# The first weight pieces of a sub-layer: an own slab for the first, a new order of low parts and normalisations, half pieces, and unread products

## The chip, the cores and the metric

The kernel runs on one core of a Trainium2 chip. The metric is the device time of one execution in microseconds. PE is TensorE, DVE is VectorE, ACT is ScalarE, POOL is GpSimd, and SP is the SyncE queue that issues the transfers of weights.

## The reference, cut to what matters

One decoder layer over 256 tokens of 2048 channels, batch 1, all in fp32: three sub-layers, each modulated by products of the condition `c` with `w_cond`.

```python
mod = (silu(c) @ w_cond + b_cond).reshape(B, 3, 3, 2048)     # shift, scale, gate of each sub-layer
u = x * (1 + mod[:, 0, 1]) + mod[:, 0, 0]
h = (silu(u @ w1) * (u @ w3)) @ w2                            # FFN1, inner width 5632
x = layer_norm(ALPHA * x + 0.5 * (1 + mod[:, 0, 2]) * h)
u = x * (1 + mod[:, 1, 1]) + mod[:, 1, 0]
q, k, v, s = split(u @ w_in)                                  # mixer
h = concat([diff_attention(q, k, v), s5(s)]) @ w_out
x = layer_norm(ALPHA * x + (1 + mod[:, 1, 2]) * h)
...                                                           # FFN2 as FFN1, then the output
```

## The kernel before, in words

**Products.** An fp32 operand is held as two rounded parts, `hi` and `lo` for weights, `Uh` and `Ul` for activations (`Hh`/`Hl`, `Ah`/`Al` further on). A product is three on PE: hi with Uh, hi with Ul, lo with Uh.

**The stream.** Weights come in pieces of 128 x 1024 (512 KB), one `Job` each, in one fixed order over all three sub-layers. SP loads a piece into a ring of four `raw` buffers (`load_to`). `split_to(k)` lets ACT write `hi` (a cast) for all pieces up to number k and puts the subtraction that makes `lo` on a list; `pay` lets DVE work that list off, and after each issues the load of one more raw buffer. The rings of hi and lo have four buffers each. After each job, `split_to(done + 4)` runs and `drain` adds DVE work that has time: `gv`, a multiply-and-sum of `c` with a 128 x 1024 piece of `w_cond`. How much is added follows `GVM`, a share of PE's time. The order of each engine's instructions is exactly the order in which this program issues them; an engine that waits holds everything behind it.

**A boundary between sub-layers.** The last block of columns (`last_block`) is done for token half 0 over all pieces, then for token half 1 in two parts, so that half 0's residual (`r`, `Y`), statistics and normalisation run beside half 1's products. Half 0 is normalised on ACT, half 1 on DVE, 512 columns at a time (four `TENSOR_SCALAR` on `Y`); `NOW` says how many of the four are done at once. Then `turn` transposes Y (products with `ident`): for a pair of 128-column blocks (k), first of token half 0, then of token half 1. `put` makes the operands from the transposed block: ACT writes `uf`, ACT or DVE casts it to `Uh`, DVE subtracts to `Ul`. The first two turns cover k 0 to 3, and "turn 2" and "turn 3" below cover k 4 and 5, and 6 and 7. After the first two turns come the first jobs of the next sub-layer, with later turns between them.

**First jobs.** The mixer begins with 16 jobs for `s` (`mk_s`); one job multiplies 128 columns of weights with k 0 to 7 (24 products 256 wide), so job 0 of the mixer needs turns 2 and 3, which are called in the midst of it by `between`. An FFN job multiplies two k with 512 columns (12 products 512 wide): jobs 0 and 1 need k 0 and 1, jobs 2 and 3 need k 2 and 3.

**Other names.** `slab` is a pool of twelve 128 x 2048 buffers; `pslab` is one of a phase. `Z_AT` is a table of the jobs after which Y gets its residual input (the `SCALAR_TENSOR_TENSOR Y<-X,Y`); `QUIET` is the number of last jobs of a sub-layer that run without the limit on DVE work. At the start, 32 narrow products of `early` with `scT` make the first shift, before any U is there.

Of the kernel before, what the change touches and what calls it, by code (L numbers as in the profile page):

```python
# [37 lines left out]
GV_RING = 52  # L38
NT2 = 20
LIM = (3.0, 100.0, 100.0, 100.0)  # L40
GVM = (0.57, 0.65, 0.85, 0.4)
LAG = 8.0
S5_WAIT = 1.7
BG_AT = 70
# [8 lines left out]
S5_AT = 17  # L53
S5_STEP = 4
X_AT = (239, 240, 244, 250)
Z_AT = (242, 246, 251, 256)
NOW = (4, 4)
QUIET = 3
RW = (8, 3, 64)
MAGIC = 12582912.0  # L60
NEG = -1.0e30
# [56 lines left out]
def tile_layer(tc, A, out):  # L118
    nc = tc.nc
    V, S, PE, SP, GP = Meter(nc.vector), nc.scalar, Meter(nc.tensor), nc.sync, nc.gpsimd  # L120
    with ExitStack() as ctx:
# [8 lines left out]
        def psum():  # L130
            return psp.tile([128, 512], F32, tag="ps", name="ps")
# [38 lines left out]
        for k, v in shapes.items():  # L170
# [9 lines left out]
        scT = small([128, NK], "scT", 1)  # L180
        onesr = small([1, 128], "onesr", 5, F32R, tag="w1")
        V.tensor_copy(onesr, ones)
        ch, cl = ([ring.tile([128, CH], F32R, tag=n, name="c" + n, bufs=AHEAD)[0:1, :] for _ in range(2)]
                  for n in ("hi", "lo"))
        for h in range(2):
# [18 lines left out]
        st = {"raw": RAW, "split": 2, "lim": None, "gv_max": 0.0, "gv_credit": 0.0, "s5_at": 0.0}  # L204

        gv_order = [(u, kt) for u in UNITS for kt in range(NS)]
        gv_tiles, gv_n = {}, {"load": 0, "done": 0, "cap": NS}
# [21 lines left out]
        def gv_step():  # L231
            n = gv_n["done"]
            gv_load(n + (8 if n < GV_RING else GVB))
            t = gv_tiles.pop(n)
            u, j = gv_order[n]
            if j == 0:
                st["acc"] = small([128, NS], "acc")
                if n < GV_RING:
                    V.memset(st["acc"], 0.0)
            w = t.shape[-1]  # L240
            gv_n["done"] += w // 1024
            if n == 0:
                st["shift"] = p = psum()[:, 0:1]
                for k in range(NK):
                    PE.matmul(p, t[:, k * 128:(k + 1) * 128], scT[:, k:k + 1], start=k == 0, stop=k == NK - 1)
            else:
                c0 = 0 if w > 1024 else j % 2 * 1024
                V.scalar_tensor_tensor(out=t, in0=t, scalar=1.0, in1=sc[:, c0:c0 + w], op0=ALU.mult, op1=ALU.mult,
                                       accum_out=st["acc"][:, j:j + 1])
                pay_late()  # L250
            n, j = gv_n["done"] - 1, j + w // 1024 - 1
            if n < 4 * NS and j % 8 == 7:
                finish(u, st["acc"], j // 4 - 1, j // 4 + 1)
            elif n >= 4 * NS and j == NS - 1:
                gv_end(u, st.pop("acc"))
# [138 lines left out]
        def pslab(name, dt=F32):  # L394
            return st["ph"].tile([128, D], dt, tag="pslab", name=name)
# [264 lines left out]
        class Stream:  # L660
            def __init__(self):
                self.jobs, self.q, self.raws, self.parts = [], [], {}, {}
                self.ld = self.sp = self.done = 0
                self.limit = 10 ** 6
                self.due, self.owed = {}, []

            def later(self, n, f):
                self.due.setdefault(self.done + n, []).append(f)
# [12 lines left out]
            def split_to(self, k, whole=True):  # L681
                while self.sp < min(k, len(self.q), self.limit):
                    self.load_to(self.sp + 1)
                    raw = self.raws.pop(self.sp)
                    if len(self.q) - 6 <= self.sp < len(self.q) - 4:
                        x = pslab("hilo", F32R)
                        hi, lo = x[:, 0:CH], x[:, CH:2 * CH]
                    else:
                        hi = ring.tile([128, CH], F32R, tag="hi", name="hi", bufs=AHEAD)
                        lo = ring.tile([128, CH], F32R, tag="lo", name="lo", bufs=AHEAD)  # L690
                    S.copy(hi, raw)  # L691
                    self.owed.append((lo, raw, hi))
                    self.parts[self.sp] = (hi, lo)
                    self.sp += 1
                    if whole:
                        self.pay()
# [41 lines left out]
        def kx(tiles, k, t0=0, t1=T):  # L738
            return tiles[k // 8][:, (k % 8) * T + t0:(k % 8) * T + t1]
# [12 lines left out]
        def between(k):  # L752

            if k in mid:
                mid.pop(k)()
# [30 lines left out]
        def last_block(B, ops, db, sub):  # L786

            held = []

            def mk(k0, first, last, src, hold=True):  # L790
                def mm(hi, lo):
                    if first:
                        B["pd"], B["whole"] = [psum(), (psum(), psum())], True
                    form_b1(B["pd"][0], hi, lo, *ops(), k0, 0, first, last)
                    held.append((hi, lo, k0))
                    if not last:
                        return
                    whole = "whole" in B
                    residual(0, db, B["pd"][0])
                    ln_token(sub, 0)  # L800
                    for j, p in enumerate(B["pd"][1]):
                        for i, (h, l, k) in enumerate(held):
                            form_b1(p, h, l, *ops(), k, 1, i == 0 and whole, i == len(held) - 1, 256 * j, 256 * j + 256)
                        if j == 1:
                            stream.split_to(stream.done + 2, False)
                        residual(1, db, p, 256 * j, 256 * j + 256)
                    held.clear()
                    ln_token(sub, 1)
                return Job(mm, src, hold=hold)
            return mk  # L810

        def halves(w, h):
            return w[:, h * CH:(h + 1) * CH]
# [65 lines left out]
            for x, n in zip(st["gb"], ("lng", "lnb")):  # L879
                SP.dma_start(x[:, cs], A[n][sub:sub + 1, cs].to_broadcast([128, 1024]))  # L880

        def turn(ks, then):

            ps = {}
            for k2 in ks:
                for t in range(2):
                    st.pop(("norm", k2 // 2, t), lambda: None)()
            for t in range(2):
                for k2 in ks:
                    if t == 0:  # L890
                        ps[k2] = psum()
                    for i in range(2):
                        PE.transpose(ps[k2][:, i * 256 + t * 128:i * 256 + (t + 1) * 128],
                                     st["Y"][t][:, (2 * k2 + i) * 128:(2 * k2 + i + 1) * 128], ident)
                    if t == 1:
                        then(k2, ps[k2])

        def turn_mod(blk):
            def then(k2, p):
# [217 lines left out]
        def mixer():  # L1117
# [12 lines left out]
            def mk_s(t, hf):  # L1130
                def mm(hi, lo):
                    if hf == 0 and t % 2 == 0:
                        M["ps", t // 2] = psum()
                    M["pt"] = p = M["ps", t // 2][:, (t % 2) * T:(t % 2 + 1) * T]
                    for k in range(8):
                        between(8 * hf + k)
                        w = hi[:, k * 128:(k + 1) * 128]
                        PE.matmul(p, w, kx(st["U"][0], 8 * hf + k), start=hf == 0 and k == 0 and t % 2 == 0,
                                  stop=False, skip_group_check=True)
                        PE.matmul(p, w, kx(st["U"][1], 8 * hf + k), start=False, stop=False, skip_group_check=True)  # L1140
                    for k in range(8):
                        PE.matmul(p, lo[:, k * 128:(k + 1) * 128], kx(st["U"][0], 8 * hf + k), start=False,
                                  stop=hf == 1 and k == 7, skip_group_check=True)

                def post():
                    s = w1([128, 4, 64], "sT")
# [4 lines left out]
                    if t % 4 == 3:  # L1151
# [3 lines left out]
                        for i in range(4):  # L1155
# [1 line left out]
                                M["U4"][32 * i:32 * i + 32, h * 1024:(h + 1) * 1024]  # L1157
                                .rearrange("p (g c) -> p g c", c=64),
                                sD[h * 512:(h + 1) * 512, i, :].rearrange("(g p) c -> p g c", p=32))
                return Job(mm, halves(A["win_a"][t], hf), post if hf else None)  # L1160

            def mk_qk(h, which, hf):
                def mm(hi, lo):
# [327 lines left out]
                 ffn(A["f2w13"], A["f2w2"], 6, [(0, 8), (8, 16)], NT2, KEEP[1])]  # L1491
        for p in parts:
            stream.add(p)
        st["U"] = pairs("U")
        xT = [slab("xT"), slab("xT")]

# [62 lines left out]
        stream.run(4 * NT1 - BG_AT)  # L1559
        bg5.extend(rest)  # L1560
        new_stats()
        stream.run(len(parts[0]) - 4 * NT1 - QUIET)
        drain_s5()
        st["lim"] = None
        stream.run(QUIET)
        stream.flush()
        open_phase("ph1")


        st["X"] = st["Y"]  # L1570
        st["U"] = pairs("U")
        turn(range(2), turn_mod(3))
        mid[2] = lambda: turn((2,), turn_mod(3))
        mid[4] = lambda: turn((3,), turn_mod(3))
        for i in range(4):
            stream.later(1 + i, lambda i=i: turn((4 + i,), turn_mod(3)))
        affines(0, slab, AFF[0])
        new_stats()
        st["lim"], st["gv_max"] = LIM[1], GVM[1]
        stream.run(len(parts[1]) - QUIET)  # L1580
        st["lim"] = None
        stream.run(QUIET)
        stream.flush()
        open_phase("ph2")

# [5 lines left out]
        def kept(k2, p):  # L1591
            q = k2 // 2
            S.copy(xT[:, (k2 % 4) * 512:(k2 % 4 + 1) * 512], p)
            if k2 % 2:
                st["xT", 6, q] = xT[:, (q % 2) * 1024:(q % 2 + 1) * 1024]
                if ("ready", 6, q) in st:
                    modulate(6, q)
        turn(range(2), turn_mod(6))
        stream.later(0, lambda: turn((2,), turn_mod(6)))
        stream.later(1, lambda: turn((3,), turn_mod(6)))  # L1600
        for i in range(4):
            stream.later(2 + i, lambda i=i: turn((4 + i,), kept))
        affines(1, pslab, AFF[1])
        new_stats()
        st["lim"], st["gv_max"] = LIM[2], GVM[2]
# [73 lines left out]
```

## Time and profile before

| | us |
|---|---|
| runs: median (lowest to highest of 3) | 1914.42 (1912.57 to 1918.12) |
| the profiled execution | 1912.22 |
| its span, first to last instruction | 1910.4 |
| PE busy | 1858.5 |
| DVE busy | 1488.1 |
| ACT busy | 889.4 |

Times in the profile are us from the start of the span. A row of the timeline gives start, duration, engine, line, operation, tiles (out<-in), shapes and the number of instructions in a row; in brackets stand the idle time of the engine ahead of it and what ended it. The recorded duration of a product overlaps the next one, so the time that a product takes is read from start to start. The two boundaries lie at about 783 (FFN1 to mixer) and 1148 us (mixer to FFN2).

### The profile page before, as it was taken

Reading aid. Unit: us, or ns where it says so; the run is one execution under the profiler, and the core shown is the slowest. Engines: PE = TensorE matmul, PEld = TensorE weight load, DVE = VectorE, ACT = ScalarE, POOL = GpSimd, SP = SyncE. Lnnn points to the kernel's source line nnn. Section 1 sums busy time; section 2 is a strip of 40 time slices with the busy share of each in tenths; the row PEclk is TensorE's granted clock in tenths of the full one; section 3 lists DMA queues with packets and bytes.
Section 4 is the critical chain, followed back from the end, with each engine's and each line's share of the span. In section 5 each row is a group of like instructions: output and inputs, shape, how many; then the busy total and the mean of one; then the engine's idle time right before and its main releaser. Section 6 shows DMA issues by size and latency. Waiting matters only on the chain.

```text
span 1910.4 us, 25429 instructions
## 1 busy us (share of the span) xinstructions
PE 1858.5 (97%) x9326; PEld 1567.5 (82%) x9326; DVE 1488.1 (78%) x2255; ACT 889.4 (47%) x1211; POOL 65.0 (3%) x119
## 2 busy tenths in 40 slices
PE   6999999999999999899999998999999999999996
PEld 5888878888888888889999886888888888888885
DVE  6889899978888979888998987887876555445468
ACT  3544444465445433634457635544444444344442
POOL 0000000000000000111210000000000000000000
PEclk9999999999999999999999998999999999999998
DMA  9999878889899888798988885998887555565563
GB/s 375 363 338 315 296 247 292 295 306 309 305 347 326 308 323 312 280 337 294 313 268 311 283 309 202 339 357 275 294 279 249 187 188 191 194 215 187 191 233 110
DMA packets 151935, 532.36 MB, mean 279 GB/s; under 512 B 21841, under 2 KB 23297, under 8 KB 150657
## 3 DMA queue, kind: packets, MB, share of 16 engines
q1 hardware_dynamic: 137234, 495.32, 74.3%
q0 software_dynamic: 6512, 23.89, 3.7%
q10 hardware_dynamic: 8064, 11.54, 1.7%
q8 instruction: 73, 1.20, 0.2%
q14 instruction: 52, 0.43, 0.1%
HBM read 513.34 MB, written 17.33 MB: 278 GB/s over the span
## 4 chain that ended last, share of the span: by engine, by line
PE 87%; DVE 6%; DMA 4%; ACT 2%; issue 1%; POOL 0%; SPq 0%; DVEq 0%; ACTq 0%; POOLq 0%
PE ps L106 87%; DVE lo L106 2%; DVE Y L106 2%; DMA raw<-in_f1w_dram 1%; DVE gv L106 1%; ACT hi L691 1%; DMA early<-in_w_cond_dram 1%; DMA raw<-in_wout_dram 0%; DMA U<-sD 0%; DVE st L106 0%; DVE r L106 0%; DMA sD<-sT 0%; DMA early<-in_wc_dram 0%; ACT Y L865 0%; DVE early L106 0%
## 5 line engine op out<-in xcount | busy, mean ns | idle before, releaser
L106 DVE TENSOR_TENSOR lo<-raw,hi 128x1024 fp32r<-128x1024 f32 x630 | 766.3, 1222 | 342.1 <-ACT hi L691 338.5
L691 ACT CAST hi<-raw 128x1024 fp32r<-128x1024 f32 x630 | 661.4, 1053 | 705.8 <-PE ps L106 461.0
L106 PE MATMUL ps<-hi,Uh 128*128 128x512 f32 x1472 | 583.7, 397 | 16.7 <-ACT Uh L318 9.7
L106 PE MATMUL ps<-hi,Ul 128*128 128x512 f32 x1472 | 577.5, 392 | 0.8 <-DVE Ul L106 0.8
L106 PE MATMUL ps<-lo,Uh 128*128 128x512 f32 x1472 | 457.4, 392 | 1.3 <-DVE lo L106 1.3
L106 PEld LDWEIGHTS ps<-hi,Uh 128*128 128x128 f32 x1472 | 278.7, 189 | 77.8 <-ACT Uh L318 10.4
L106 PEld LDWEIGHTS ps<-lo,Uh 128*128 128x128 f32 x1472 | 278.4, 189 | 60.9 <-DVE lo L106 2.0
L106 PEld LDWEIGHTS ps<-hi,Ul 128*128 128x128 f32 x1472 | 279.0, 190 | 58.1 <-DVE Ul L106 1.9
L106 DVE SCALAR_TENSOR_TENSOR gv<-gv,sc 128x1024 f32<-128x1024 f32 x258 | 314.2, 1219 | 1.4 <-DMA gv<-in_w_cond_dram 1.3
L106 PE MATMUL ps<-hi,Hh 128*128 128x512 f32 (+1 forms) x716 | 274.6, 385 | 0.0
L106 PE MATMUL ps<-hi,Hl 128*128 128x512 f32 (+1 forms) x716 | 273.6, 383 | 0.0
L106 PE MATMUL ps<-lo,Hh 128*128 128x512 f32 (+1 forms) x716 | 216.5, 384 | 1.8 <-DVE lo L106 1.8
L106 PEld LDWEIGHTS ps<-lo,Hh 128*128 128x128 f32 x716 | 133.0, 188 | 29.1 <-DVE lo L106 2.6
L106 PEld LDWEIGHTS ps<-hi,Hh 128*128 128x128 f32 x716 | 134.5, 188 | 26.8 <-issue 0.4
L106 PEld LDWEIGHTS ps<-hi,Hl 128*128 128x128 f32 x716 | 134.6, 188 | 26.0
L106 PE MATMUL ps<-Uh,hi 128*128 128x256 f32 x384 | 97.9, 292 | 2.4 <-ACT sT L1147 1.8
L106 PE MATMUL ps<-Ul,hi 128*128 128x256 f32 x384 | 95.7, 286 | 0.1
L106 PEld LDWEIGHTS ps<-Uh,hi 128*128 128x128 f32 x384 | 74.2, 193 | 6.2 <-ACT sT L1147 2.7
L106 PEld LDWEIGHTS ps<-Ul,hi 128*128 128x128 f32 x384 | 74.2, 193 | 0.8 <-DVE Ul L106 0.7
L1010 ACT CAST Hh<-ps 128x512 fp32r<-128x512 f32 x44 | 25.8, 587 | 78.6 <-PE ps L106 78.6
L106 PE MATMUL ps<-Uh,lo 128*128 128x256 f32 x384 | 53.9, 283 | 0.0
L106 DVE TENSOR_TENSOR Hl<-ps,Hh 128x512 fp32r<-128x512 f32 x44 | 30.3, 688 | 30.0 <-ACT Hh L1010 29.7
(229 smaller groups left out, 1393.4 us busy)
## 6 DMA issues: line engine op xcount, KB each, us to landing
raw<-in_f1w_dram SPq DMA_DIRECT2D x264, 512.0 KB, 6.0
raw<-in_f2w_dram SPq DMA_DIRECT2D x264, 512.0 KB, 4.7
gv<-in_w_cond_dram SPq DMA_DIRECT2D x258, 512.0 KB, 7.1
raw<-in_win_a_dram SPq DMA_DIRECT2D x48, 512.0 KB, 6.0
raw<-in_wout_dram SPq DMA_DIRECT2D x32, 512.0 KB, 5.8
early<-in_w_cond_dram SPq DMA_DIRECT2D x28, 512.0 KB, 7.6
s5m<-scrB POOLq DMA_DIRECT2D x8, 1024.0 KB, 8.4
raw<-in_win_v_dram SPq DMA_DIRECT2D x16, 512.0 KB, 4.8
```

The lines of the kernel that those rows point to most:

```text
L106: return f(*a, **k)
L691: S.copy(hi, raw)
L1010: S.copy(hh, p)
```

## The change

Five things change. (1) `warm(n)` issues n products 128 x 512 of a small constant tile `wr` into a PSUM buffer that nothing reads: 16 in the opening, and at each boundary 11 or 12 between the transposes of token half 0 and those of half 1, and 3 behind the latter. (2) The first piece of the mixer and of FFN2 (`firsts`) gets hi and lo in a slab of its own, `hilo`, ahead of the last residual of half 0, and one piece more is cast by ACT at the second part of half 1. (3) `first_turn` replaces the first two turns: of half 1 only the first 512 columns are normalised before them; then follow the lo of job 1's piece, the second normalisation, the casts and lo's of the next pieces, and the last two normalisations. (4) In the mixer the first four jobs do k 0 to 3, with turns 2 and 3 behind the second and third, and then k 4 to 7 of all four; turns 4 to 7 come two jobs later, and in FFN2 every later turn one job later. (5) `Z_AT`, `QUIET` and `GVM` get other numbers.

```diff
-GVM = (0.57, 0.65, 0.85, 0.4)
+GVM = (0.57, 0.68, 0.85, 0.4)
-Z_AT = (242, 246, 251, 256)
-NOW = (4, 4)
-QUIET = 3
+Z_AT = (242, 246, 250, 254)
+NOW = (4, 1)
+QUIET = (6, 5)
+S_LATER = 3
+WARM = dict(opening=16, mixer=(11, 3), ffn=(12, 3))
...
+        def warm(n):
+            p = psum()
+            for _ in range(n):
+                PE.engine.matmul(p, wr[:, 0:1].to_broadcast([128, 128]), wr.unsqueeze(1).to_broadcast([128, 16, 32]),
+                                 start=True, stop=True)
...
                 for k in range(NK):
                     PE.matmul(p, t[:, k * 128:(k + 1) * 128], scT[:, k:k + 1], start=k == 0, stop=k == NK - 1)
+                warm(WARM["opening"])
...
-                    if len(self.q) - 6 <= self.sp < len(self.q) - 4:
-                        x = pslab("hilo", F32R)
+                    if len(self.q) - 6 <= self.sp < len(self.q) - 4 or self.sp in self.firsts:
+                        x = (slab if self.sp in self.firsts else pslab)("hilo", F32R)
...
                     whole = "whole" in B
+                    stream.split_to(stream.done + 2)
                     residual(0, db, B["pd"][0])
...
                         if j == 1:
-                            stream.split_to(stream.done + 2, False)
+                            stream.split_to(stream.done + 3, False)
...
+        def first_turn(blk, idle):
+            turn(range(2), turn_mod(blk), idle)
+            stream.pay()
+            st.pop(("norm", 1, 1))()
+            stream.split_to(stream.done + AHEAD)
+            for q in (2, 3):
+                st.pop(("norm", q, 1))()
...
+                    if hf or t >= AHEAD:
+                        some(p, hi, lo, range(8), hf == 0 and t % 2 == 0)
+                        return
+                    some(p, hi, lo, range(4), t % 2 == 0)
+                    M.setdefault("held", []).append((p, hi, lo))
+                    between(t)
+                    if t == AHEAD - 1:
+                        for i, x in enumerate(M.pop("held")):
+                            some(*x, range(4, 8), False)
+                            stream.split_to(stream.done + 2 + i)
...
-        turn(range(2), turn_mod(3))
-        mid[2] = lambda: turn((2,), turn_mod(3))
-        mid[4] = lambda: turn((3,), turn_mod(3))
+        first_turn(3, WARM["mixer"])
+        mid[1] = lambda: turn((2,), turn_mod(3))
+        mid[2] = lambda: turn((3,), turn_mod(3))
         for i in range(4):
-            stream.later(1 + i, lambda i=i: turn((4 + i,), turn_mod(3)))
+            stream.later(S_LATER + i, lambda i=i: turn((4 + i,), turn_mod(3)))
...
-        turn(range(2), turn_mod(6))
-        stream.later(0, lambda: turn((2,), turn_mod(6)))
-        stream.later(1, lambda: turn((3,), turn_mod(6)))
+        first_turn(6, WARM["ffn"])
+        stream.later(1, lambda: turn((2,), turn_mod(6)))
+        stream.later(2, lambda: turn((3,), turn_mod(6)))
```

On PE at boundary 2, before, the transposes follow one another and job 0 has a hi and lo of the ring:

```order
L106 MATMUL ps_10805<-ident_76,Y_2700 128x128 [waits Activation_49]
L106 MATMUL ps_10805<-ident_76,Y_2700 128x128
L106 MATMUL ps_10808<-ident_76,Y_2700 128x128 x2
L106 MATMUL ps_10805<-ident_76,Y_2701 128x128 [waits DVE_49]
L106 MATMUL ps_10805<-ident_76,Y_2701 128x128
L106 MATMUL ps_10808<-ident_76,Y_2701 128x128 x2
L106 MATMUL ps_10836<-hi_10772,Uh_10800 128x512 [waits DVE_49]
```

At the same place of the changed kernel (Y_2719 is token half 0, Y_2720 half 1):

```order
L108 MATMUL ps_10841<-ident_76,Y_2719 128x128 [waits Activation_49]
L108 MATMUL ps_10841<-ident_76,Y_2719 128x128
L108 MATMUL ps_10844<-ident_76,Y_2719 128x128 x2
L216 MATMUL ps_10847<-wr_98 128x512 x12
L108 MATMUL ps_10841<-ident_76,Y_2720 128x128 [waits DVE_49]
L108 MATMUL ps_10841<-ident_76,Y_2720 128x128
L108 MATMUL ps_10844<-ident_76,Y_2720 128x128 x2
L216 MATMUL ps_10880<-wr_98 128x512 x3
L108 MATMUL ps_10904<-hilo_10730,Uh_10836 128x512 [waits DVE_49]
```

The unread products stand where PE had nothing to do, and job 0 reads its weights from the slab.

On ACT behind boundary 2, before, from the second put on (uf_10855 is turn 2's; the three hi that follow are of jobs 1 to 3):

```order
L743 ACTIVATE uf_10827<-ps_10808,bt6_135,gs6_132 128x256
L745 CAST Uh_10800<-uf_10827 128x256 [waits Activation_49]
L743 ACTIVATE uf_10855<-ps_10850,bt6_135,gs6_132 128x256 [waits PE_49]
L743 ACTIVATE uf_10859<-ps_10850,bt6_135,gs6_132 128x256 [waits DVE_49]
L745 CAST Uh_10800<-uf_10859 128x256 [waits Activation_49]
L691 CAST hi_10863<-raw_10607 128x1024 [waits DMAHW7_49]
L691 CAST hi_10869<-raw_10631 128x1024 [waits DMAHW0_49]
L691 CAST hi_10875<-raw_10666 128x1024 [waits DMAHW2_49]
```

And in the changed kernel (hi_10888 to hi_10918 are of jobs 2 to 4, uf_10946 is turn 2's):

```order
L755 ACTIVATE uf_10876<-ps_10844,bt6_137,gs6_134 128x256
L757 CAST Uh_10836<-uf_10876 128x256 [waits Activation_49]
L703 CAST hi_10888<-raw_10676 128x1024 [waits DMAHW1_49]
L703 CAST hi_10894<-raw_10704 128x1024 [waits DMAHW3_49]
L703 CAST hi_10918<-raw_10733 128x1024 [waits DMAHW4_49]
L755 ACTIVATE uf_10946<-ps_10941,bt6_137,gs6_134 128x256 [waits PE_49]
```

The casts stand ahead of turn 2's uf instead of behind it.

On DVE at the end of FFN1, before, between the last but one and the last residual of token half 0 (r_6654):

```order
L106 SCALAR_TENSOR_TENSOR Y_2700<-X_6148,Y_2700 128x512 [waits DMAHW0_49]
L106 SCALAR_TENSOR_TENSOR Y_2701<-X_6149,Y_2701 128x512 [waits DMAHW1_49]
L106 TENSOR_TENSOR lo_6574<-raw_6485,hi_6573 128x1024 [waits DMAHW5_49,Activation_49]
L106 TENSOR_TENSOR lo_6601<-raw_6503,hi_6600 128x1024 [waits DMAHW6_49,PE_49,Activation_49]
L106 TENSOR_TENSOR lo_6625<-raw_6524,hi_6624 128x1024 [waits DMAHW0_49,PE_49,Activation_49]
L106 TENSOR_TENSOR r_6654<-ps_6579,G_6147 128x512 [waits PE_49]
```

In the changed kernel:

```order
L108 TENSOR_TENSOR lo_6593<-raw_6504,hi_6592 128x1024 [waits DMAHW5_49,Activation_49]
L108 TENSOR_TENSOR lo_6620<-raw_6524,hi_6619 128x1024 [waits DMAHW6_49,PE_49,Activation_49]
L108 TENSOR_TENSOR lo_6644<-raw_6547,hi_6643 128x1024 [waits DMAHW0_49,PE_49,Activation_49]
L108 TENSOR_TENSOR hilo_6673<-raw_6565,hilo_6673 128x1024 [waits DMAHW1_49,Activation_49]
L108 TENSOR_TENSOR r_6678<-ps_6598,G_6166 128x512 [waits PE_49]
```

The two operations on Y have gone to a place further up, and the slab's lo stands ahead of r.

More of the change, by code (lines that the diff above doesn't have):

```diff
@@ L182, in tile_layer @@
         V.tensor_copy(onesr, ones)
+        wr = sb.tile([128, 32], F32R, tag="wr", name="wr")
+        V.tensor_copy(wr, ident[:, 0:32])
         ch, cl = ([ring.tile([128, CH], F32R, tag=n, name="c" + n, bufs=AHEAD)[0:1, :] for _ in range(2)]
@@ L664, in __init__ @@
                 self.limit = 10 ** 6
-                self.due, self.owed = {}, []
+                self.due, self.owed, self.firsts = {}, [], ()
             def later(self, n, f):
@@ L880, in load_affine, with turn @@
                 SP.dma_start(x[:, cs], A[n][sub:sub + 1, cs].to_broadcast([128, 1024]))
-        def turn(ks, then):
+        def turn(ks, then, idle=(0, 0)):
             ps = {}
@@ L896, in turn @@
                         then(k2, ps[k2])
+                if idle[t]:
+                    warm(idle[t])
+        def first_turn(blk, idle):
[5 more added lines that the diff above has]
+                st.pop(("norm", q, 1))()
         def turn_mod(blk):
@@ L1134, in mm, with some @@
                     M["pt"] = p = M["ps", t // 2][:, (t % 2) * T:(t % 2 + 1) * T]
[L1135 to L1143, printed above, removed]
+                    def some(p, hi, lo, ks, first):
+                        for k in ks:
+                            w = hi[:, k * 128:(k + 1) * 128]
+                            PE.matmul(p, w, kx(st["U"][0], 8 * hf + k), start=first and k == 0, stop=False,
+                                      skip_group_check=True)
+                            PE.matmul(p, w, kx(st["U"][1], 8 * hf + k), start=False, stop=False, skip_group_check=True)
+                        for k in ks:
+                            PE.matmul(p, lo[:, k * 128:(k + 1) * 128], kx(st["U"][0], 8 * hf + k), start=False,
+                                      stop=hf == 1 and k == 7, skip_group_check=True)
+                    if hf or t >= AHEAD:
[8 more added lines that the diff above has]
+                            stream.split_to(stream.done + 2 + i)
                 def post():
@@ L1159, in post @@
                                 sD[h * 512:(h + 1) * 512, i, :].rearrange("(g p) c -> p g c", p=32))
-                return Job(mm, halves(A["win_a"][t], hf), post if hf else None)
+                return Job(mm, halves(A["win_a"][t], hf), post if hf else None, hold=not hf and t < AHEAD - 1)
             def mk_qk(h, which, hf):
@@ L1493, in tile_layer @@
             stream.add(p)
+        stream.firsts = (len(parts[0]), len(parts[0]) + len(parts[1]))
         st["U"] = pairs("U")
@@ L1561, in tile_layer @@
         new_stats()
-        stream.run(len(parts[0]) - 4 * NT1 - QUIET)
+        stream.run(len(parts[0]) - 4 * NT1 - QUIET[0])
         drain_s5()
         st["lim"] = None
-        stream.run(QUIET)
+        stream.run(QUIET[0])
         stream.flush()
@@ L1579, in tile_layer @@
         st["lim"], st["gv_max"] = LIM[1], GVM[1]
-        stream.run(len(parts[1]) - QUIET)
+        stream.run(len(parts[1]) - QUIET[1])
         st["lim"] = None
-        stream.run(QUIET)
+        stream.run(QUIET[1])
         stream.flush()
@@ L1597, in kept @@
                     modulate(6, q)
-        turn(range(2), turn_mod(6))
-        stream.later(0, lambda: turn((2,), turn_mod(6)))
-        stream.later(1, lambda: turn((3,), turn_mod(6)))
+        first_turn(6, WARM["ffn"])
+        stream.later(1, lambda: turn((2,), turn_mod(6)))
+        stream.later(2, lambda: turn((3,), turn_mod(6)))
         for i in range(4):
-            stream.later(2 + i, lambda i=i: turn((4 + i,), kept))
+            stream.later(3 + i, lambda i=i: turn((4 + i,), kept))
         affines(1, pslab, AFF[1])
```

## The prediction

> **What bounds the kernel now.** I read the page's busy line and shares of the chain first, then the table of TensorE's waits, then each place where a wait is long, in the timeline.
>
> ```profile
> PE 1858.5 (97%) x9326; PEld 1567.5 (82%) x9326; DVE 1488.1 (78%) x2255; ACT 889.4 (47%) x1211; POOL 65.0 (3%) x119
> PE 87%; DVE 6%; DMA 4%; ACT 2%; issue 1%; POOL 0%; SPq 0%; DVEq 0%; ACTq 0%; POOLq 0%
> ...
> PE ps L106 <- ACT Uh L318: 9.7, 2, 7.6
> PE ps L106 <- DVE Y L106: 6.3, 2, 3.2
> ```
>
> PE is busy 97% of the span and 87% of the chain, so only its waits, and products that run at a low clock, can be saved. A wait's numbers are us in total, times, longest. The two on Y are the two boundaries between sub-layers; 7.6 of the other row is the opening. What a boundary costs beyond its waits stands in windows: us, then busy time of PE, PEld, DVE, ACT, POOL, the granted clock, DMA share, GB/s.
>
> ```profile
> 1160.00:1165.00 5.00, 2.51 (x9) 1.82 (x8) 2.79 (x5) 4.04 (x6) 0.00 (x0) 0.50 0.00 0
> 1165.00:1170.00 5.00, 5.00 (x18) 3.90 (x17) 3.04 (x4) 1.81 (x4) 0.00 (x0) 0.62 0.73 217
> ...
> 1148.29:1151.70 3.41, 0.39 (x4) 0.40 (x4) 2.91 (x11) 1.73 (x3) 0.00 (x0) 1.00 0.03 11
> 35.56:38.98 3.42, 1.33 (x7) 0.79 (x5) 3.31 (x10) 2.22 (x4) 0.00 (x0) 1.00 1.03 404
> 844.50:847.90 3.40, 2.06 (x18) 1.86 (x16) 2.27 (x2) 2.10 (x2) 0.00 (x0) 1.00 1.03 262
> ```
>
> The first two rows are the start of FFN2: PE runs at half clock there, half of the time idle. In them and around them the granted clock changes only at moments that lie whole steps of 3.41 us apart (38.98, 1151.70 and 1168.76 among them), so the other three rows are stretches of 3.4 us that end at such moments. At the end of the first and second, 11% and 39% busy, the clock fell; at the end of the third, 61% busy, it stayed. So a stretch well over half busy seems to keep the clock, and one under 40% to lose it.
>
> **Boundary 2, mixer to FFN2.** PE's rows (start, us, idle before in brackets), then ACT, DVE and SP:
>
> ```profile
> 1151.31 0.78 PE L106 MATMUL ps<-ident,Y 128*128 128x128 f32 x4 [3.23 <-DVE Y L106]
> 1152.88 0.80 PE L106 MATMUL ps<-hi,Uh 128*128 128x512 f32 x1 [0.79 <-DVE Uh L106]
> 1156.25 1.22 PE L106 MATMUL ps<-lo,Uh 128*128 128x512 f32 x2 [1.27 <-DVE lo L106]
> 1163.38 0.79 PE L106 MATMUL ps<-hi,Uh 128*128 128x512 f32 x1 [2.49 <-ACT hi L691]
> 1163.97 0.63 PE L106 MATMUL ps<-hi,Ul 128*128 128x512 f32 x1
> 1164.40 0.63 PE L106 MATMUL ps<-hi,Uh 128*128 128x512 f32 x1
> 1174.22 0.40 PE L106 MATMUL ps<-hi,Uh 128*128 128x512 f32 x1
> 1174.45 0.39 PE L106 MATMUL ps<-hi,Ul 128*128 128x512 f32 x1
> 1175.14 0.60 PE L106 MATMUL ps<-ident,Y 128*128 128x128 f32 x4
> 1175.49 0.48 PE L106 MATMUL ps<-hi,Uh 128*128 128x512 f32 x1
> ...
> 1162.29 3.88 ACT L691 CAST hi<-raw 128x1024 fp32r<-128x1024 f32 x4
> 1150.70 1.91 DVE L106 TENSOR_SCALAR Y<-Y,mv,rs 128x512 f32<-128x512 f32 x4
> 1154.98 1.22 DVE L106 TENSOR_TENSOR lo<-raw,hi 128x1024 fp32r<-128x1024 f32 x1
> 1156.27 9.80 SPq L677 DMA_DIRECT2D raw<-in_f2w_dram  x3
> ```
>
> From start to start a 512-wide product takes 0.43 us cold (1163.97 to 1164.40) and 0.23 warm (1174.22 to 1174.45). The second group of transposes is let go by the first of the four normalisations. Twelve unread products take 12 x 0.23 = 2.8 us and fit in the 3.23 idle; the stretch is then over 80% busy, so I expect full clock. Taking three of four normalisations away frees DVE 1.4 us earlier, and the first Uh comes some 0.3 earlier: first product at about 1152.6. Job 0 finds hi and lo in the slab, so the wait of 1.27 goes; its 12 products take 2.75, plus a little for Ul: 1155.8. Job 1's hi is cast before the boundary as job 0's was; its lo is the first thing on DVE after the puts, ready at about 1155.9, and is wanted at 1156.7: it ends at 1158.55. Turn 2 takes 0.35 (1175.14 to 1175.49), job 2 ends at 1161.65, turn 3 and job 3 at 1164.75. Their hi casts no longer stand behind turn 2's uf on ACT, so the wait of 2.49 goes; on DVE their lo follow by 1158.8. Before, job 3 ended at 1175.14, with one turn more (0.35): 1175.14 - 0.35 - 1164.75 = **10.0 us**. If instead the clock falls at 1151.70 as now, job 0 takes 12 x 0.43 = 5.1 to 1158.0; the stretch from 1155.12 is full, so the clock is up at 1158.53, and jobs 1 to 3 end at 1167.2: 7.6. So most of the gain rests on the waits, and I keep 7.6 to 10.0. Next late are the raw loads, which wait in SP's queue until DVE's lo frees a buffer (1156.27): job 5's is then issued at about 1155.9, wanted at 1167.5.
>
> **Boundary 1, FFN1 to mixer.**
>
> ```profile
> 786.71 1.11 PE L106 MATMUL ps<-ident,Y 128*128 128x128 f32 x4 [3.06 <-DVE Y L106]
> 788.40 0.58 PE L106 MATMUL ps<-Uh,hi 128*128 128x256 f32 x1 [0.58 <-DVE Uh L106]
> 795.84 0.28 PE L106 MATMUL ps<-Ul,hi 128*128 128x256 f32 x1
> 795.96 0.28 PE L106 MATMUL ps<-Uh,hi 128*128 128x256 f32 x1
> 805.23 0.60 PE L106 MATMUL ps<-ident,Y 128*128 128x128 f32 x4
> ...
> 786.11 2.04 DVE L106 TENSOR_SCALAR Y<-Y,mv,rs 128x512 f32<-128x512 f32 x4
> 788.07 0.28 DVE L106 CAST Uh<-uf 128x256 fp32r<-128x256 f32 x1
> 790.62 1.22 DVE L106 TENSOR_TENSOR lo<-raw,hi 128x1024 fp32r<-128x1024 f32 x1
> 795.01 3.50 DVE L106 TENSOR_TENSOR lo<-raw,hi 128x1024 fp32r<-128x1024 f32 x3 [0.52 <-ACT hi L691]
> ```
>
> Eleven unread products take 2.5 of the idle 3.06. First Uh at about 787.75, first product 788.07. Here DVE sets the pace, because the four first pieces need every k of U before they can end, and the lo's now come between. From 787.75: the puts of k 0 to 3 as now (788.07 to 790.62) 2.55, one lo 1.17 (3.50/3), a normalisation 0.5 (2.04/4), two lo 2.3, two normalisations 1.0, the puts of k 4 to 7 2.55: 797.85. PE meanwhile has done the first halves. After the last Ul it has five products of 0.12 (795.84 to 795.96) for job 0 and 36 for the other second halves: 0.6 + 4.3, job 3 ends at 802.8. Before, it ended at 805.23 with turns 4 and 5 inside, 0.7: **1.7 us** gained. The bounds: with no wait at all, 4 x 24 x 0.12 plus two turns from 788.07 end at 800.3, a gain of 4.2; and between 788.07 and 790.6 only eight products of 0.12 run, a stretch perhaps half busy, between the 39% that lost the clock and the 61% that kept it. Lost from 789.9 for two stretches of 3.4, it costs up to 3.4: -1.7. I take 1.7, since the three unread products behind the transposes stand in that stretch too.
>
> That last bound is where a rule bears on the trace: by the 39% row the stretch may lose the clock, and the sum below would be 10.1; the 61% row would leave it at 13.5. The Trainium skill, "TensorE: Matmul & The Clock Gate", Part 1: The HAM clock gate, states that the throttle comes back after at least one idle window of about 3.4 us, the windows running free. By that rule a stretch with eight products in it is safe, and 13.5 stands. The steps of 3.41 us agree with it; that the window must be idle does not, since one of 39% lost the clock.
>
> **The lo's ahead of the last r.**
>
> ```profile
> 773.97 0.72 PE L106 MATMUL ps<-lo,Hh 128*128 128x512 f32 x2 [1.20 <-DVE lo L106]
> 771.50 1.28 DVE L106 SCALAR_TENSOR_TENSOR Y<-X,Y 128x512 f32<-128x512 f32 x2
> 777.49 0.69 DVE L106 TENSOR_TENSOR r<-ps,G 128x512 f32<-128x512 f32 x1 [1.31 <-PE ps L106]
> 1883.99 0.73 PE L106 MATMUL ps<-lo,Hh 128*128 128x512 f32 x2 [0.58 <-DVE lo L106]
> ...
> 810.00:1140.00 330.00, 325.86 (x2264) 300.31 (x2264) 291.92 (x503) 168.12 (x311) 30.93 (x55) 1.00 0.89 302
> ```
>
> At the end of FFN1 two operations of 1.28 together stood ahead of the lo that PE waited 1.20 for; with Z_AT and QUIET they come earlier: **1.2 us**; the same at the end of FFN2, **0.6**. The slab's lo (1.22) stands ahead of r, which had 1.31 idle: covered, and without that cover it costs 1.2. The earlier raw load of the slab's piece takes one buffer of four sooner; the products of w_cond stay as many and move within the mixer, where PE idles 4.1 us of 330 in all (last row): 0, and 1 us either way.
>
> **The opening.** Here PE's wait is for ACT's Uh, which hangs on transfers.
>
> ```profile
> 22.75 0.79 PE L106 MATMUL ps<-hi,Uh 128*128 128x512 f32 x1 [7.59 <-ACT Uh L318]
> 28.59 0.46 PE L106 MATMUL ps<-hi,Ul 128*128 128x512 f32 x1
> 38.86 0.74 PE L106 MATMUL ps<-hi,Uh 128*128 128x512 f32 x1 [2.09 <-ACT Uh L318]
> ```
>
> Sixteen unread products, even cold 16 x 0.43 = 6.9 us, fit in 7.59. The products are cold from 22.75 to 28.59, whose duration of 0.46 lies between cold and warm; warm, they would be done 2.9 us sooner (half of 5.84), and wait as much longer at 38.86 for the same Uh, in the stretch of 39% above, with DMA share 1.03: 0, at best 2.9.
>
> **Sum.** 10.0 + 1.7 + 1.2 + 0.6 = 13.5 us. The profiled execution took 1912.2 (span 1910.4): 1898.7. The median of the runs is 1914.42, 2.2 above: 1900.9, said as 1901. Best bounds, 10.0 + 4.2 + 1.8 + 2.9 = 18.9, give 1895.5; worst, 7.6 - 1.7 + 0.6 = 6.5, 1907.9.
>
> **Rivals.**
> *The clock falls at a boundary all the same* (because transposes or unread products don't keep it): 7.6 instead of 10.0 at the second, -1.7 at the first: 1903 to 1908. For it: the 39% row. Against: after the change no stretch at boundary 2 is under 60% busy. By the Trainium skill, the same page, Part 4: PE-mode transpose, transposes don't count as busy; no row here tells them apart.
> *The opening gains too*: 1898. For it: the cold products to 28.59. Against: the waits at 38.86.
> *The gain is given back at once*: FFN2 starts 10 us earlier on raw loads that SP can't issue sooner than lo frees buffers. If jobs 5 to 8 each wait 2.5 us, boundary 2 keeps nothing and 3.5 are left: 1911. Against: 12 us between issue and need.
> *Slower*: DVE becomes late in the mixer, 810 to 1140, where it is the engine next to PE; the budget of w_cond products rises by .68/.65, about 3 products of 1.22. It decides where DVE's share passes PE's; 16 lo's late by 1.2 each take 19 us and end at 1920. For it: DVE is 88% busy there (291.92 of 330). Against: PE is 99% busy there, and the products of w_cond are as many.
>
> **Numbers.** As forecast 0.60 (1897 to 1904), clock 0.18, opening 0.08, given back 0.09, slower 0.05. A difference under 0.3% (5.7 us) can't be told from none. Faster 0.86, same 0.09, slower 0.05; range 1896 to 1908.
>
> **What would show it.** Right: clock 1.0 from 1148 on, job 3 of FFN2 ending 10 us sooner against the end of the mixer, no waits on hi or lo at the boundaries, and a wait on Uh near 38.86 as long as before or longer. Wrong: a clock of 0.5 at either place, waits of PE on lo or raw in FFN2's first ten jobs, or new waits on lo in the mixer.

## The result

| | before | changed |
|---|---|---|
| median of 5 runs, us | 1914.42 (1910.42 to 1920.72) | 1903.43 (1901.29 to 1906.43) |
| profiled execution, us (span) | 1912.22 (1910.4) | 1905.15 (1903.3) |

The ratio is 0.9936, 95% interval 0.9916 to 0.9957: faster by 11.0 us in the medians, where 13.5 were forecast (1901, range 1896 to 1908). The two profiled executions differ by 7.1 us only, and it is in them that one sees where the time went. I cut each at the first transposes of token half 0 at the two boundaries, and a boundary's own interval goes from there to the start of the ninth job behind it, when all turns are done in both kernels.

| us | before | changed | difference | forecast |
|---|---|---|---|---|
| start to boundary 1 | 783.05 | 783.72 | +0.7 | -1.2 |
| boundary 1, to its ninth job | 34.56 | 32.77 | -1.8 | -1.7 |
| the rest of the mixer | 329.87 | 333.58 | **+3.7** | 0 |
| boundary 2, to its ninth job | 39.98 | 30.49 | -9.5 | -10.0 |
| the rest of FFN2 (to PE's last product) | 708.31 | 708.16 | -0.2 | -0.6 |

The table of PE's waits in the changed kernel (us in total, times, longest):

```profile
PE ps L108 <- ACT Uh L330: 4.2, 2, 2.7
...
PE ps L108 <- DMA s5e<-scrA: 2.3, 1, 2.3
...
PE ps L108 <- DVE sg L108: 1.6, 3, 1.1
PE ps L108 <- DVE Y L108: 1.1, 2, 0.7
...
PE ps L108 <- DVE lo L108: 0.2, 1, 0.2
```

The two waits on Y have shrunk from 6.3 to 1.1 and those on lo from 3.6 to 0.2; a new one, for a transfer into `s5e`, has come. The timeline of PE at boundary 2, the rows that answer to those of before (products left out at each `...`):

```profile
1150.07 0.60 PE L108 MATMUL ps<-ident,Y 128*128 128x128 f32 x4
1150.43 3.07 PE L216 MATMUL ps<-wr 128*128 128x512 f32 x12
1153.92 0.66 PE L108 MATMUL ps<-ident,Y 128*128 128x128 f32 x4 [0.42 <-DVE Y L108]
1154.33 0.95 PE L216 MATMUL ps<-wr 128*128 128x512 f32 x3
1155.34 0.50 PE L108 MATMUL ps<-hilo,Uh 128*128 128x512 f32 x1
...
1158.55 0.39 PE L108 MATMUL ps<-hi,Uh 128*128 128x512 f32 x1
...
1161.27 0.60 PE L108 MATMUL ps<-ident,Y 128*128 128x128 f32 x4
...
1164.48 0.60 PE L108 MATMUL ps<-ident,Y 128*128 128x128 f32 x4
...
1167.70 0.60 PE L108 MATMUL ps<-ident,Y 128*128 128x128 f32 x4
```

The unread products fill the idle time but for 0.42, none of the waits on lo and hi is left, and from job 1 on PE runs without a gap: job 1 takes 2.72 us (1158.55 to 1161.27), where it took 5.3 before (1163.38 to 1168.66). At boundary 1 the rows are these; job 3 ends 19.52 us behind the first transposes (783.72 to 803.24), where it ended 22.18 behind them before, with two turns more inside:

```profile
783.72 0.60 PE L108 MATMUL ps<-ident,Y 128*128 128x128 f32 x4
784.08 2.84 PE L216 MATMUL ps<-wr 128*128 128x512 f32 x11
787.64 0.65 PE L108 MATMUL ps<-ident,Y 128*128 128x128 f32 x4 [0.72 <-DVE Y L108]
...
803.24 0.60 PE L108 MATMUL ps<-ident,Y 128*128 128x128 f32 x4
```

The mixer's loss has one main place. First PE's row, then three rows of POOL in the changed kernel, then the same of the kernel before, then the changed kernel's window in front of the clock's fall and the one behind it:

```profile
931.05 3.27 PE L108 MATMUL ps<-U,s5e 128*128 128x64 f32 x16 [2.33 <-DMA s5e<-scrA]
```

```profile
906.03 2.21 POOL L1232 DMA_DIRECT2D s5e<-KD  x4
923.58 0.54 POOL L313 DMA_DIRECT2D growD<-grow  x1 [15.34 <-DVE grow L108]
924.11 0.57 POOL L1229 DMA_DIRECT2D s5e<-scrA  x1
```

```profile
908.68 2.21 POOL L1197 DMA_DIRECT2D s5e<-KD  x4
919.13 0.54 POOL L301 DMA_DIRECT2D growD<-grow  x1 [8.24 <-DVE grow L106]
919.66 0.57 POOL L1194 DMA_DIRECT2D s5e<-scrA  x1
```

```profile
928.10:931.52 3.42, 1.09 (x10) 0.86 (x9) 3.39 (x7) 2.77 (x6) 0.93 (x2) 1.00 1.07 423
931.52:934.93 3.41, 3.41 (x20) 3.29 (x21) 3.36 (x10) 0.00 (x0) 0.00 (x0) 0.50 1.01 331
```

POOL issues in program order. The store of the gate row, `growD<-grow` (16 products of w_cond, turned and written to memory for the residual of the mixer), stands ahead of the load for the next S5 step. Before, DVE had the row at 919, the load was issued at 919.66 and came in time. In the changed kernel the row comes at 923.58, the load goes out 4.5 us later, PE waits 2.33 for it, and with the stretch up to 931.52 only 32% busy the clock falls for two steps of 3.41 us: 3.2 us more. That U<-sD, 2.3 before, was not waited for in this execution takes 2.2 off again.

A smaller loss of 0.7 lies in the ninth job itself. On DVE a product of w_cond (`gv`) stands ahead of the last turn's Uh and Ul, and PE, here its weight loads (PEld), waits for both:

```profile
816.60 1.22 DVE L108 SCALAR_TENSOR_TENSOR gv<-gv,sc 128x1024 f32<-128x1024 f32 x1
...
817.75 0.29 DVE L108 CAST Uh<-uf 128x256 fp32r<-128x256 f32 x1
818.07 0.76 DVE L108 TENSOR_TENSOR Ul<-uf,Uh 128x256 fp32r<-128x256 f32 x2
```

```profile
818.09 0.19 PEld L108 LDWEIGHTS ps<-Uh,hi 128*128 128x128 f32 x1 [0.20 <-DVE Uh L108]
818.55 0.19 PEld L108 LDWEIGHTS ps<-Ul,hi 128*128 128x128 f32 x1 [0.27 <-DVE Ul L108]
```

Followed product by product against the kernel before, the rest of the mixer loses 0.7 here, wins 2.2 at U<-sD, loses 5.7 around the wait on s5e and wins 0.4 at its end: the 3.7 of the table.

### The profile page after: what moved, and what is told of

It is laid out like the page before. It is cut to its first block, busy times and chain, and to the rows that moved or that the text cites. A ratio compares the mean times of both kernels' runs of the same rounds, so it can differ in the third digit from the quotient of the medians.

```text
span 1903.3 us, 25525 instructions
## 1 busy us (share of the span) xinstructions
PE 1866.7 (98%) x9371; PEld 1572.7 (83%) x9371; DVE 1488.6 (78%) x2256; ACT 889.6 (47%) x1211; POOL 65.3 (3%) x119
## 4 chain that ended last, share of the span: by engine, by line
PE 83%; DVE 8%; DMA 5%; ACT 2%; issue 2%; SPq 0%; POOL 0%; DVEq 0%; ACTq 0%
PE ps L108 83%; DMA raw<-in_f1w_dram 2%; DVE lo L108 2%; DVE gv L108 2%; DVE Y L108 1%; DMA early<-in_w_cond_dram 1%; ACT hi L703 1%; DMA raw<-in_wout_dram 1%; DVE early L108 0%; DMA s5e<-scrA 0%; DVE st L108 0%; DVE r L108 0%; DMA early<-in_wc_dram 0%; ACT Y L878 0%; DMA yD<-y 0%
```

## The experiments

Twelve runs, each profiled (again and changed_beside are the changed kernel, grow_later_beside is grow_later); "rest" is the mixer behind its ninth job. A median of one run is marked *; ratios are to the kernel before on the same chip, whose medians were 1915.41 (first four rows), 1914.58 (next four) and 1914.20 (last four).

| kernel | median us | ratio (95%) | boundary 1 | rest | boundary 2 |
|---|---|---|---|---|---|
| again | 1908.33* | | 32.75 | 336.21 | 30.51 |
| grow_later | 1900.08 | 0.9927 (0.9912 to 0.9942) | 32.77 | 329.65 | 31.00 |
| no_unread | 1907.69 | 0.9963 (0.9944 to 0.9981) | 34.45 | 330.49 | 31.96 |
| only_unread | 1912.83 | 0.9986 (0.9977 to 0.9995) | 33.66 | 329.40 | 36.87 |
| no_slab | 1907.09 | 0.9963 (0.9949 to 0.9976) | 33.63 | 332.77 | 34.19 |
| whole_pieces | 1907.72 | 0.9957 (0.9942 to 0.9972) | 39.44 | 329.43 | 30.47 |
| norms_first | 1904.31* | | 32.60 | 334.56 | 30.47 |
| old_tables | 1903.64 | 0.9940 (0.9920 to 0.9959) | 32.77 | 331.77 | 30.81 |
| changed_beside | 1904.52 | 0.9949 (0.9935 to 0.9963) | 32.76 | 333.95 | 30.43 |
| grow_later_beside | 1901.25 | 0.9927 (0.9913 to 0.9941) | 32.75 | 328.83 | 31.03 |
| s5_later | 1908.45 | 0.9967 (0.9954 to 0.9980) | 32.76 | 335.62 | 30.45 |
| double_unread | 1911.22 | 0.9985 (0.9973 to 0.9996) | 34.41 | 337.36 | 32.68 |

The intervals of the boundaries repeat within 0.1 us from one execution of a kernel to the next; the rest of the mixer and FFN1 do not (the changed kernel's three profiles have 781.0 to 784.3 us up to boundary 1). So a part's worth is read from the intervals, and the medians are the check. The intervals of the kernel before come from one execution only.

**again** and **grow_later**: the queue.

> The changed kernel once more, unaltered. In its profile the mixer held one surprise: PE waited 2.33 us for the transfer s5e<-scrA at 931, the clock then fell for 6.8 us, together some 5.5 us. Theory Q (POOL's queue): the store of the gate row, growD<-grow, now stands ahead of that load in POOL's fixed order and waits for DVE until 923.6 (before: 919.1); then the wait and the cold stretch come again within 0.5 us. Theory J (chance of transfers): the wait is under 0.5 us and the clock stays up. For the drift of 1.9 us in FFN1 (waits on sg): chance gives a first boundary between 782 and 785, an effect of the change 783.5 to 784.

The wait on s5e was 2.0 and the clock fell at 933.4 for 6.8 us, as theory Q has it. Boundary 1 came at 784.3, outside what an effect of the change would give, and at 781.0 in changed_beside: the drift in FFN1 is chance. The execution took 1908.33, more than any of the five before it.

```diff
-            gv_later(DL + 4, turned)
-            gv_later(DL + 5, store)
+            gv_later(DL + (8 if blk == 5 else 4), turned)
+            gv_later(DL + (9 if blk == 5 else 5), store)
```

> The changed kernel with the gate row of the mixer turned and stored four jobs later, so that its store stands behind the s5e load instead of ahead of it; nothing else moves. Theory Q: no wait for s5e at 931, clock 1.0 through the mixer, 2.3 + 3.2 = 5.5 us less: mixer stretch (first transposes of boundary 1 to those of boundary 2) 361 us instead of 366.4, the whole some 1898. Theory J: within 1 us of the changed kernel, 1903.

The wait is gone (PE's waits between 790 and 1130 of grow_later):

```profile
PE ps L108 <- ACT sT L1182: 1.9, 4, 0.5
PE ps L108 <- DMA U<-sD: 1.2, 1, 1.2
PE ps L108 <- DVE Y L108: 0.7, 1, 0.7
```

The rest of the mixer takes 329.65 instead of 333.58 and 336.21, and the whole 1900.08. Boundary 2 gives 0.5 back in both executions of this kernel: the raw of the slab's piece landed later, so that its lo, with 1.35 us idle ahead of it, held the last r; it used up the cover that the prediction named. The mixer stretch was 362.4, not 361.

**changed_beside** and **grow_later_beside**: the same two kernels side by side.

> The changed kernel, timed beside the next one on the same chip. Theory Q expects a median of 1903 to 1907 and the wait on s5e at about 931 with the clock lower behind it.

> The changed kernel with the gate row stored four jobs later, once more. Theory Q: 3 to 6 us below the median of the changed kernel beside it, no wait on s5e. Theory J: the same within 1 us.

3.3 us between the medians: Q, at the low end. In this execution of the changed kernel the wait on s5e was only 0.9 and cost no clock; a wait of 1.86 for U<-sD at 845 did (846.1 to 852.9). So this pair of profiles doesn't show the 3.3; the medians do, whose five runs each don't overlap (1902.72 to 1906.07 against 1898.19 to 1901.87). POOL's rows of grow_later_beside show the load issued ahead of the row now:

```profile
906.33 2.22 POOL L1232 DMA_DIRECT2D s5e<-KD  x4
908.54 0.56 POOL L1229 DMA_DIRECT2D s5e<-scrA  x1
...
939.29 0.54 POOL L313 DMA_DIRECT2D growD<-grow  x1 [12.30 <-DVE grow L108]
```

**no_unread** and **only_unread**: the clock against the waits.

```diff
-WARM = dict(opening=16, mixer=(11, 3), ffn=(12, 3))
+WARM = dict(opening=0, mixer=(0, 0), ffn=(0, 0))
...
+            if not n:
+                return
```

> The changed kernel without any unread product. Theory W (the waits carry the gain): the clock falls at both boundaries for two steps of 3.41 us; boundary 2 keeps about 7.6 of its gain (measured with unread products 9.4), boundary 1 loses 0 to 1.5 since DVE paces it; the whole 2 to 4 us above the changed kernel. Theory C (the clock carries it): boundary 2 keeps less than 5 us, five steps or more at half clock as before, the whole 6 us or more above. Opening: no difference in either.

only_unread is the kernel before with `wr`, `warm` and its calls in the opening and in the first two turns of each boundary, and nothing else.

> The kernel before with nothing but the unread products added (16, 11 and 3, 12 and 3). Theory W: the waits on lo (1.27) and hi (2.49) at boundary 2 stay, since their causes do; the clock holds there, so that FFN2's first four jobs end about 5 us sooner than before, half of what the whole change gains there; boundary 1 gains 1 to 3 us, its products being warm, and DVE the pace. The whole 4 to 8 us below the kernel before. Theory C: nearly all of the gain of the changed kernel, 9 us or more at boundary 2. A third way: the clock falls in the wait on hi, the gain under 3 us.

Without unread products boundary 2 keeps 8.0 of its 9.5 us, and the clock is down for one step only (from 1154.5), since job 0 and 1 follow without a wait; boundary 1 loses 1.7 of its 1.8, more than theory W had, with the clock down for two steps (789.3 to 796.1). With nothing but unread products boundary 2 gains 3.1 and boundary 1 0.9, and the whole 2.6, each less than theory W had. There the clock does not fall at 1151; it falls later, at the third way's place, in the waits that were left:

```profile
1154.88 0.73 PE L107 MATMUL ps<-lo,Uh 128*128 128x512 f32 x2 [1.94 <-DVE lo L107]
1159.93 0.71 PE L107 MATMUL ps<-hi,Uh 128*128 128x512 f32 x1 [2.49 <-ACT hi L701]
```

The window before the fall at 1160.1, a quarter busy:

```profile
1156.70:1160.10 3.40, 0.91 (x7) 0.58 (x6) 1.34 (x4) 2.59 (x5) 0.00 (x0) 0.99 0.27 102
```

The opening is the same with and without: its 144th product with U started at 64.8 in the changed kernel, 65.3 in no_unread, 64.4 before. In PE's timeline of the changed kernel the 0.7 us won by the wait (the last product ahead of it starts at 35.67, before at 36.39) is waited out at 38.75; the unread products did not keep the clock there either, it fell at 23.6 for one step:

```profile
15.02 6.32 PE L216 MATMUL ps<-wr 128*128 128x512 f32 x16
22.89 0.49 PE L108 MATMUL ps<-hi,Uh 128*128 128x512 f32 x1 [1.55 <-ACT Uh L330]
...
38.75 0.51 PE L108 MATMUL ps<-hi,Uh 128*128 128x512 f32 x1 [2.69 <-ACT Uh L330]
```

**double_unread**: what a product in excess costs.

```diff
-WARM = dict(opening=16, mixer=(11, 3), ffn=(12, 3))
+WARM = dict(opening=16, mixer=(22, 3), ffn=(24, 3))
```

> The changed kernel with 22 and 24 unread products between the transposes instead of 11 and 12. Theory (an unread product is free only in idle time): 11 and 12 left 0.72 and 0.42 us of idle, so 11 x 0.23 - 0.72 = 1.8 and 12 x 0.23 - 0.42 = 2.3 us later transposes, and PE bound behind boundary 2: boundary 2 32.8 instead of 30.5, boundary 1 34.6 instead of 32.8. Rival: the lateness is made up, since DVE goes on with low parts meanwhile: under 0.5 us each.

34.41 and 32.68, that is 1.6 and 2.2 us more: the excess over the idle time is paid, but for 0.2 and 0.1 of what the theory had. (The whole, 1911.2, is above that sum; its mixer fell cold in two places, at 851 and 937.)

**no_slab**: the first piece back in the rings.

```diff
-                    stream.split_to(stream.done + 2)
...
-                            stream.split_to(stream.done + 3, False)
+                            stream.split_to(stream.done + 2, False)
...
-        stream.firsts = (len(parts[0]), len(parts[0]) + len(parts[1]))
```

> The changed kernel without the own slab: the first piece of the mixer and of FFN2 is cast into the rings at the second part of token half 1, and its lo comes behind the puts, as before; everything else as changed. Intervals are read from the first transposes of a boundary to the start of the ninth job behind it: before 34.56 (boundary 1) and 39.98 (boundary 2), changed 32.77 and 30.49. Theory S (each wait is worth its length): PE waits again about 1.3 us for job 0's lo at boundary 2, and its lo (1.2) joins the DVE chain at boundary 1: 31.8 and 34.0. Rival: the wait is only moved, since job 1's lo is later by the same 1.2 and job 0's products could wait for Ul anyway: boundary 2 stays under 31.0.

Boundary 1 33.6, near the 34.0 of theory S; boundary 2 34.2, which is more than either says: 3.7 us for the slab and the place of its lo. The wait is longer than before, because PE comes to it sooner (its first product starts 5.08 us behind the transposes instead of 5.40, and at full clock) while the lo is ready no sooner, and the window with it lost the clock (1159.8, one step):

```profile
1159.32 0.80 PE L108 MATMUL ps<-lo,Uh 128*128 128x512 f32 x2 [2.00 <-DVE lo L108]
```

```profile
1156.40:1159.80 3.40, 1.40 (x5) 0.78 (x6) 3.18 (x7) 3.37 (x6) 0.00 (x0) 1.00 0.00 0
```

**whole_pieces**: the halves undone.

```diff
-                    if hf or t >= AHEAD:
+                    if hf == 0 and t == 0:
+                        for k in range(8):
+                            between(k)
...
+                    if True:
...
-                return Job(mm, halves(A["win_a"][t], hf), post if hf else None, hold=not hf and t < AHEAD - 1)
+                return Job(mm, halves(A["win_a"][t], hf), post if hf else None)
...
-        mid[1] = lambda: turn((2,), turn_mod(3))
-        mid[2] = lambda: turn((3,), turn_mod(3))
+        mid[2] = lambda: turn((2,), turn_mod(3))
+        mid[4] = lambda: turn((3,), turn_mod(3))
```

> The changed kernel with the mixer's first four pieces whole again: job 0 runs k 0 to 7 with turns 2 and 3 in its midst, as before; the order on DVE (low parts and normalisations ahead of the puts of k 4 to 7) stays. Theory P (halves give PE work while DVE catches up): job 0 stands still from k 3 on until DVE has done two lo's and three normalisations more, 4 to 5 us, and the clock falls in it: boundary 1 takes 37 to 40 us instead of 32.8, worse than before (34.6). Rival (halves bring nothing, DVE paces both): 32.5 to 33.5. Boundary 2 unchanged at 30.5.

39.44, theory P: PE stands 2.35 for the normalisation ahead of turn 2 and 0.99 for Uh behind it, and the clock is down for three steps (790.4 to 800.6). So the new order on DVE without the halves would make boundary 1 4.9 us slower than before.

```profile
791.30 0.69 PE L108 MATMUL ps<-ident,Y 128*128 128x128 f32 x2 [2.35 <-DVE Y L108]
...
794.69 0.58 PE L108 MATMUL ps<-Uh,hilo 128*128 128x256 f32 x1 [0.99 <-DVE Uh L108]
```

The mixer's start has no three held jobs here, each job adds its products again, and the gate row is stored at 918.4: no wait on s5e in this kernel.

**norms_first**: all normalisations ahead.

```diff
-NOW = (4, 1)
+NOW = (4, 4)
...
-            st.pop(("norm", 1, 1))()
-            for q in (2, 3):
-                st.pop(("norm", q, 1))()
```

> The changed kernel with all four normalisations of token half 1 ahead of the first turns, as before. They hold DVE for 1.4 us longer; the first Uh, 1.9 us behind the start of the normalisation, needs DVE at about the same time. Theory S: first products 0 to 0.3 us later, then the two lo's behind come earlier by as much as the normalisations no longer stand between: boundary 1 32.5 to 33.0, boundary 2 30.4 to 30.9. Rival: the order of normalisations carries much of the gain: 1 us or more at either boundary.

32.60 and 30.47: theory S. This part of the change is worth nothing at the boundaries; the wait on s5e (1.8) stays.

**old_tables**: the old numbers of Z_AT, QUIET and GVM.

```diff
-GVM = (0.57, 0.68, 0.85, 0.4)
+GVM = (0.57, 0.65, 0.85, 0.4)
...
-Z_AT = (242, 246, 250, 254)
+Z_AT = (242, 246, 251, 256)
...
-QUIET = (6, 5)
+QUIET = (3, 3)
```

> The changed kernel with the old numbers of Z_AT, QUIET and GVM. Theory S: the waits of 1.20 at 774 and 0.58 at 1884 on lo come back, and one of about 0.6 at the mixer's end; both boundary intervals as changed. For the gate row: with the smaller budget its 16 products end later still, so the wait on s5e at 931 and the fall of the clock stay or grow (theory Q); if they vanish, the budget was their cause and not the four jobs without fresh products at the mixer's start. The whole within 3 us of the changed kernel.

At FFN2's end the wait came back with 1.2, and that stretch took 709.43 instead of 708.16. At FFN1's end none came back, though the two operations on Y stand ahead of the lo again, and none at the mixer's end. The 0.7 us of the ninth job are not lost here: with the smaller budget no product of w_cond stands ahead of the last turn on DVE. And the wait on s5e is gone, for a reason that none of the expectations had: the gate row is later still, so late that its store falls *behind* the load in program order (931.03, with the load at 910.96). What is bad is a late store ahead of the load; a still later one behind it does no harm. PE waited 3.6 for U<-sD in this execution instead.

**s5_later**: an attempt at a better version.

```diff
-S5_AT = 17
+S5_AT = 18
```

(on top of grow_later)

> As the last, and every step of the S5 branch one job later (S5_AT 18 instead of 17). PE waited 0 to 3.6 us for the transfer U<-sD at the first of these steps in the ten profiles so far (mean 1.5), with the length of the wait left to the transfers. Theory: one job is 2.9 us of cover, the wait is under 0.5 us, the whole 1 to 2 us below the last kernel. Rival: the later steps now fall on other jobs than before, DVE is late for some lo, and the gain is gone: same or slower.

The wait on U<-sD is gone, and the rival has it all the same: 1908.45, 7.2 above grow_later_beside. DVE is late with the S5 steps at their new places (PE waits twice on s5e from DVE, 2.2 us in all), and the clock falls at 944.2 and 995.4, three steps of 3.41 in all. The best version tried is grow_later: 1900.08 and 1901.25. Three parts of the change were tried by no run alone: the casts of hi ahead of turn 2, the later turns, and the one piece more that ACT casts; what they are worth is inside the totals.

## Why the prediction was right or wrong

- **Boundary 2, 10.0 forecast, 9.5 measured: right**, and by its mechanism. no_unread gives 8.0 where the bound with a cold clock was 7.6. The first product was said to come 0.3 us sooner for the three normalisations taken away; it came 0.1 sooner (5.27 us behind the transposes instead of 5.40; at boundary 1 5.34 and 5.35), since uf on ACT, not DVE, set it: DVE idled 1.13 ahead of that Uh.
- **Boundary 1, 1.7 forecast, 1.8 measured: right.** DVE paces it as described: its last Ul of k 0 to 7 ends at 798.17, 14.45 us behind the transposes, where the sum has 14.8. The clock held in the sparse stretch, and it matters: without the unread products 1.7 of the 1.8 go. That the ninth job then loses 0.7 to a product of w_cond is in no term of the sum.
- **1.2 at FFN1's end: wrong.** The step took the wait of 1.20 in one profile for the work of the order on DVE. In only_unread and old_tables, which have the old order there, no such wait appears; in the profile of before DVE had idled 0.16 for a hi cast just ahead, that is for a transfer. So it seems to be one execution's chance. At FFN2's end the same step held: 0.6, 1.7 and 1.2 us of wait in the three profiles with the old tables, none in the others. Between the two profiles of the table FFN2's rest differs by 0.2 only.
- **"The products of w_cond stay as many and move within the mixer: 0, and 1 us either way": wrong, and the largest miss.** Their number is the same (66 in the mixer), but their *consumer* moves: the three held jobs at the mixer's start add no fresh products, the larger GVM does not quite make up for it, the gate row comes 4.5 us later, and its store stands ahead of a load in POOL's queue. The prediction named SP's queue and not POOL's. It cost 3.3 us in medians side by side; in the single profiles the wait and the cold steps behind it cost from 1.2 (changed_beside) to 5.8.
- **The opening, 0: right**, with less to it than was thought: the products were to be done 2.9 us sooner and were so by 0.7, since the clock fell at 23.6. Where it held (old_tables, whole_pieces, s5_later among others) the 144th product with U still starts at 64.6 to 64.9.
- **The size.** 13.5 less 1.2, 0.5, 0.7 and 3.3 is 7.8; the two profiles say 7.1, the medians 11.0 and, in changed_beside, 9.7. The runs of one kernel spread by 3 to 10 us, so what is between can't be placed. That the median came within 2.5 us of the forecast is therefore in part luck: the two boundaries were right, but terms of some 5 us beside them were not.
- Of the rivals, the clock fell at neither boundary and no raw load was late behind boundary 2. DVE was late in the mixer only in the ninth job (0.7). What I had as a slower way, DVE late in the mixer, is what s5_later shows.

## What to carry to other kernels

When work on one engine is delayed, follow its result to the last queue that it passes: a store that waits for it, in a queue that issues in program order, holds every load behind it; here a store that came 4.5 us late ahead of a load cost more than one that came later still, behind it. At a change of stages remove the waits first and fill what idle time is left with unread products, no more of them than fit: here, at boundary 2, the order kept 8.0 of 9.5 us without them, while they alone gained 3.1. At boundary 1, where DVE sets the pace, they were nearly all of the gain (1.7 of 1.8). A wait seen in one profile is a term of a sum only if a second execution has it too.

## What the runs showed of the hardware

A short wait of PE can cost more than its length, and whether it does depends on where it lies in the free-running steps of 3.41 us. In the fourteen profiles (before, changed and the twelve above; the last 30 us left out), worked out from all records of PE between two steps, every one of the 26 steps that were under 46% busy lost the clock; between 46% and 62% some lost it and some kept it. Four steps that were 68% to 76% busy by the records lost it as well, and all four lie at S5 steps, whose products are only 64 wide; busy time there seems not to count in full. Counting the columns of the products that start in a step, instead of recorded time, bears this out: all 40 falls followed a step with at most 3072 columns (six products 512 wide), all 31 steps under 2432 lost the clock, between the two 9 lost it and 32 kept it, and no step with more lost it. Some products can be missing from a trace, so the two bounds are rough. One of the four, of s5_later:

```profile
940.80:944.20 3.40, 2.62 (x23) 2.58 (x23) 3.35 (x9) 0.22 (x1) 0.71 (x2) 1.00 0.75 247
```

Against it, from the changed kernel's execution beside, a wait of 1.86 that cost two cold steps, 6.8 us at half clock:

```profile
842.70:846.10 3.40, 1.54 (x15) 1.37 (x13) 1.01 (x1) 0.68 (x1) 0.00 (x0) 1.00 1.03 390
846.10:852.90 6.80, 6.80 (x34) 6.80 (x34) 2.37 (x3) 0.37 (x1) 3.14 (x5) 0.50 1.02 365
```

The Trainium skill, "TensorE: Matmul & The Clock Gate", Part 1: The HAM clock gate, has the clock return to half after an idle window of about 3.4 us; in these runs a window need be idle only by somewhat more than half. Unread products between the transposes kept it: no step with them there lost the clock. Those of the opening did not always: the step from 20.2 to 23.6 in the changed kernel, in which four of them start, did.
